# A streaming mixer layer on one core: parts of the weights kept in DRAM, one LayerNorm moved to the vector engine, and a bias added by DMA

## The chip, the cores and the metric

The program runs on one core of a Trainium2 chip. The metric is the device time of one execution in microseconds (us), as the median of several runs. TensorE (PE in the profile) does the matrix products, VectorE (DVE) and ScalarE (ACT) the elementwise work that may read PSUM, GpSimd (POOL) elementwise work in SBUF, and SyncE (SP) issues the DMAs in a queue of its own. Each engine runs its instructions in the order in which they stand.

## The reference

One post-norm layer over 2048 new frames and 8 running streams of 16 frames (17 token tiles of 128). One projection `w_in` (1024 x 2816) feeds three branches; their gated outputs are concatenated, projected by `w_out` (1024 x 1024), added to the residual and normalised.

```
h = x @ w_in ;  a, g_a, u, v, g_b, c1, c2, g_c = split(h)
y_a = pool_mixer(a)                                  # trailing means, then a small product
v_n = layer_norm(v, gmlp_ln_g, gmlp_ln_b)            # an output for the running streams
y_b = u * (tril(W_s) @ v_n + b_s)                    # chunks of 128 frames, 4 heads
y_c = pointwise(silu(layer_norm(conv31(c1 * sigmoid(c2)))))
out = concat(silu(g_a)*y_a, silu(g_b)*y_b, silu(g_c)*y_c) @ w_out + b_out
x_new = layer_norm(ALPHA * x + out, ln_g, ln_b)
```

## The kernel before, in words

All of it is float32. A product is made of three one-pass products: each operand is split into a high and a low part (`hi + lo` is the operand exactly), and `mm3` (L183 to L195) issues hi x hi, lo x hi and hi x lo for each of 8 k-tiles. `split` (L150) makes the parts: a copy on ACT (`hi`, L152) and a subtraction on DVE (`lo`).

The tokens are worked on in three blocks of 6, 6 and 5 tiles. A block goes through eight column groups of `w_in` in this order: c2/c1 (two groups), ga/a (two groups of two column tiles), v, gb, u, gc. A group's weights come in four pieces of two k-tiles: `Piece` (L166) loads one into the stage (`stage`, 4 slots) and splits it into the ring (`whi`, `wlo`, 6 slots each). `Loader` (L799) keeps the stage full while the group before runs. Every block loads and splits all of `w_in` again. The tokens `xT` are loaded and split k-tile by k-tile (`XRow`, L212) while the last group of the block before runs.

The order of every engine is written by the program itself. `Clock.pe` counts TensorE's modelled time; `after(us, fn)` puts `fn` into a list of events, and `poll` calls what is due after each k-step. `fill` holds the taps of the 31-tap convolution, one DVE instruction each (`acc<-cext,cw,acc`, with `acc<-cexts,...` for the running streams in the third block): they are put into DVE's order whenever its modelled time `Clock.dve` is behind `Clock.pe`. The order fixes only what stands behind what on an engine; when an instruction starts is decided by its waits.

Branch B (`b_v`, L627): for each token tile the v product lands in PSUM (`ps_v`), DVE makes its statistics (`vst`, `vmv`), POOL makes 1/sqrt(var + eps) and -mean times it (`vrs`, `vnm`, three instructions), ACT normalises (`vn<-ps_v`, L385), and POOL multiplies by the gain and adds the offset (L649, L650). Of every run of three tiles and for each of four heads, `vn` is then split (`vhi` on ACT, `vlo` on DVE) and multiplied with the spatial weights (`ps_z`, L672). These products stand in TensorE's order among those of group gb, from 12 us of modelled time after the run's last tile on.

The output phase: the mixed branches come back from DRAM (`mix`, `Mixed` L871) and are split (`mhi`, `mlo`); w_out is split too (`woxhi`, `woxlo`, and the ring). The first two token tiles are multiplied together, k by k, then one tile after another (`ps_o`). The residual `xr` (5 buffers) is loaded, POOL adds b_out/ALPHA to it (`add_bias`, L946), which is a 128 x 1024 tile made of a broadcast load and one scaling on POOL (L926), and DVE adds the product (`xr<-xr,ps_o`); then statistics, ACT, gain and offset on DVE, and the store. Between the first tiles stands the rest of branch C of the third block (`tail_steps`: `csum`, `ps_mean`, `dc`, `csq`, `csqs`, `ps_var`, `cvar`, `crs`, `ps_rstd`).

Of the kernel before, what the change touches and what calls it, by code (L numbers as in the profile page):

```python
# [25 lines left out]
# Column tiles of 128 of the input projection.  # L26
# [23 lines left out]

# Columns of the packed per-partition constants.
# [22 lines left out]
def encoder_kernel(ctx: ExitStack, tc: tile.TileContext, a):  # L74
# [9 lines left out]
    # Every engine runs in the order given here.  # L84
    ctx.enter_context(tc.manual_schedule())

    class Clock:
        """TensorE's time as the products are given (us), and the vector engine's; what is to follow
        later waits in `events`, and the convolution's steps in `fill` for the vector engine's free time."""
# [14 lines left out]
    def drain(tag=None):  # L104
        """What is left of the convolution that `tag` names, or all of it."""
        while fill and (tag is None or any(t == tag for t, _ in fill)):
            fill.pop(0)[1]()
# [11 lines left out]
    class Vector:  # L119
        """The vector engine, with its time counted."""  # L120
# [27 lines left out]
    ring = {}  # L148

    def split(hi, lo, src, then=None):  # L150
        """src (float32) = hi + lo exactly, both in the tensor engine's one-pass type."""
# [14 lines left out]
    class Piece:  # L166
        """A load into the stage, and later its split into a piece of the weight ring."""
        def __init__(self, key, src, cols):
            self.key, self.n, self.cols = key, src.shape[1], cols
# [3 lines left out]
        def split(self, then=None):  # L173
# [3 lines left out]
            ring.setdefault(self.key, []).append((hi, lo))  # L177

# [4 lines left out]
    def mm3(outs, kdim=KT, hook=None):  # L183
        """outs: (ps, lhs, rhs); the products of both parts but for lo x lo, below float32's last bit."""
# [18 lines left out]
    def w_in(key, g):  # L203
        """The loads of a group's weights, to be made one by one."""
        w = len(GROUPS[g]) * P
        v = a["w_in"][:, gofs[g]:gofs[g] + KT * w].rearrange("p (k c) -> p k c", k=KT)
        return [lambda k0=k0: Piece(key, v[:, k0:k0 + 2, :], w) for k0 in range(0, KT, 2)]
# [4 lines left out]
    class XRow:  # L212
        """A load of one k-tile of a block's tokens, and later its split."""
        def __init__(self, b, k, mid=None):
# [6 lines left out]
            else:  # L221
                # in two parts with another load between
# [15 lines left out]
    # keeps TensorE's clock up until the first products  # L238
# [6 lines left out]
    # the first block's loads, the first two k-tiles' weights one by one  # L245
# [33 lines left out]
    # sums over the partitions, to all of them  # L279
# [3 lines left out]
    # conv weights halved, since its input is kept doubled  # L283
# [24 lines left out]
    def load_pool():  # L308
        # two groups of 64 channels on the diagonal
# [14 lines left out]
    def keep_lower(w):  # L324
        """Spatial weights [s, h, t], kept where s <= t."""
        nc.gpsimd.affine_select(out=w, in_=w, compare_op=ALU.is_ge, fill=0.0, base=0,
                                pattern=[[0, 4], [1, P]], channel_multiplier=-1)

    after(12, load_pool)
# [7 lines left out]
    def store(q, j, src):  # L337
        """Channels of a token tile's mixed branches, from channel tile j on."""
# [8 lines left out]
    # running streams' states  # L347
# [15 lines left out]
    def stats(src, npiece, nm, then):  # L363
        """Of each row: 1/sqrt(var + eps), and -mean times it, given to `then`."""
# [11 lines left out]
    def rstd(mv, nm):  # L376
        rs = const.tile([P, 1], F32, tag="rs", bufs=4, name=nm + "rs")
        nc.gpsimd.tensor_scalar(rs, mv[:, 1:2], 1.0, EPS, op0=ALU.mult, op1=ALU.add)
        nc.gpsimd.tensor_tensor(out=rs, in0=rs, in1=mhalf, op=ALU.pow)
        nm_ = const.tile([P, 1], F32, tag="nm", bufs=4, name=nm + "nm")  # L380
# [6 lines left out]
    # weights of branch C's pointwise product  # L387
# [16 lines left out]
    def c_in(b, todo, wkey, hook=None):  # L404
        """todo: (c1 or c2, channel tile, its columns in the group); with several the products go k by k."""
# [40 lines left out]
    def conv(b, j):  # L446
# [18 lines left out]
        if T > Tp:  # L465
            # the new convolution states, at their own scale
# [29 lines left out]
    def tail_steps(b):  # L496
        """The rest of branch C in pieces of TensorE's work, each a while after the one before."""
# [16 lines left out]
        def centre(i, t0, n):  # L514
            """Less the mean, which the sums over the channels give on every partition."""
# [17 lines left out]
        def variance(i, t0, n):  # L533
            """Of each token on its partition, to the power of -1/2."""
# [77 lines left out]
    def spread(steps, every=STEP):  # L612
        """One step after another, some of TensorE's time apart."""
# [11 lines left out]
    b_state = {}  # L625

    def b_v(b, wkey, hook=None):  # L627
# [4 lines left out]
        while i < len(tiles):  # L632
# [6 lines left out]
            for r, q in enumerate(run):  # L639
# [5 lines left out]
                def norm(rs, nm_, o=vn[:, r, :], ps=ps):  # L645
                    normalise(o, ps[:, :384], rs, nm_)

                    def gain():
                        nc.gpsimd.tensor_tensor(out=o, in0=o, in1=vg, op=ALU.mult)  # L649
                        nc.gpsimd.tensor_tensor(out=o, in0=o, in1=vb, op=ALU.add)  # L650
                    after(0.8, gain)
# [442 lines left out]
```

## Time and profile before

| what | value |
|---|---|
| median of three runs | 805.1 us (805.04 to 805.83) |
| span of the profiled execution | 802.9 us, so 2.2 us of the median lie outside a span like it |
| busy: PE, DVE, ACT, POOL | 778.2, 659.0, 255.0, 216.7 us |
| DMA | 88.34 MB, mean 110 GB/s |
| mean granted TensorE clock | 0.993 |
| block 1, block 2, block 3, output phase (by the products in the timeline) | about 4 to 206, 206 to 413, 413 to 589, 589 to 794 us |

The span of the profiled execution is the only time that the page has of it. In the views, a row of the table of stretches gives the stretch, its length, then for PE, PEld, DVE, ACT and POOL the busy time with the number of instructions, then the granted clock, the DMA share and GB/s. A row of a group gives busy time, the mean of one in ns, and the idle time ahead of it with what ended it. A row of the timeline gives start, length, engine, line, operation, output<-inputs and count.

### The profile page before, as it was taken

What the parts mean: (1) busy time and instruction counts of PE and PEld (TensorE: products, weight loads), DVE (VectorE), ACT (ScalarE), POOL (GpSimd) and SP (SyncE); (2) the same over time, 40 slices, a digit from 0 to 9 for tenths busy, and PEclk for the clock granted to TensorE, in tenths of its full rate; (3) what the DMA queues carried; (4) which work ended last, traced back from release to release, by engine and by line L of the source; (5) the groups of instructions that cost most, each with busy time, mean ns of one, the idle gap of its engine ahead of it and who ended that gap; (6) DMA issues with size and microseconds to landing.
All of it is one profiled execution on the core that took longest, in us unless ns stands there. A gap on an engine that the chain in (4) does not pass through costs nothing.

```text
span 802.9 us, 11388 instructions
## 1 busy us (share of the span) xinstructions
PE 778.2 (97%) x4340; PEld 734.9 (92%) x4340; DVE 659.0 (82%) x930; ACT 255.0 (32%) x457; POOL 216.7 (27%) x226
## 2 busy tenths in 40 slices
PE   8999998999999999989999999999999899999995
PEld 6999997999999999989999999999988678888885
DVE  5998989995588999999667888999777897676665
ACT  5313224314432241431354243442351233231210
POOL 1010077300002005731000201742009344232332
PEclk9999999999999999999999999999999999999998
DMA  7513311225501253111461134222575344425321
GB/s 244 162 53 109 100 60 57 64 66 170 165 28 53 73 133 97 60 40 59 136 199 47 54 83 129 83 69 86 159 236 203 124 138 158 158 108 177 121 79 64
DMA packets 50918, 88.34 MB, mean 110 GB/s; under 512 B 13616, under 2 KB 27440, under 8 KB 50864
## 3 DMA queue, kind: packets, MB, share of 16 engines
q1 hardware_dynamic: 50864, 87.62, 33.9%
q8 instruction: 34, 0.56, 0.3%
q14 instruction: 20, 0.16, 0.1%
HBM read 69.02 MB, written 18.58 MB: 109 GB/s over the span
## 4 chain that ended last, share of the span: by engine, by line
PE 70%; DVE 13%; POOL 6%; issue 4%; DMA 4%; ACT 2%; SPq 0%; POOLq 0%; DVEq 0%; ACTq 0%
PE ps_c L189 6%; PE ps_o L189 5%; PE ps_o L191 5%; PE ps_c L190 5%; PE ps_o L190 5%; PE ps_c L191 5%; DVE acc L131 4%; PE ps_u L191 3%; PE ps_u L189 3%; PE ps_u L190 3%; PE ps_gc L191 2%; PE ps_gc L189 2%; PE ps_gc L190 2%; PE ps_ga L190 2%; PE ps_ga L189 2%
## 5 line engine op out<-in xcount | busy, mean ns | idle before, releaser
L131 DVE SCALAR_TENSOR_TENSOR acc<-cext,cw,acc 128x768 f32<-128x768 f32 (+1 forms) x270 | 265.8, 984 | 4.0
L131 DVE TENSOR_TENSOR wlo<-stage,whi 128x768 fp32r<-128x768 f32 (+1 forms) x99 | 90.0, 919 | 15.8 <-ACT whi L152 15.4
L189 PE MATMUL ps_c<-xhi,whi 128*128 128x384 f32 (+1 forms) x288 | 96.1, 334 | 0.6 <-ACT xhi L152 0.6
L190 PE MATMUL ps_c<-xlo,whi 128*128 128x384 f32 (+1 forms) x288 | 94.7, 329 | 0.9 <-DVE xlo L131 0.9
L191 PE MATMUL ps_c<-xhi,wlo 128*128 128x384 f32 (+1 forms) x288 | 94.1, 327 | 0.0
L152 ACT CAST whi<-stage 128x768 fp32r<-128x768 f32 (+1 forms) x99 | 75.4, 773 | 25.3 <-PE ps_c L190 11.8
L191 PE MATMUL ps_o<-woxhi,mlo 128*128 128x512 f32 (+1 forms) x208 | 81.5, 392 | 1.8 <-DVE mlo L131 1.8
L189 PE MATMUL ps_o<-woxhi,mhi 128*128 128x512 f32 (+1 forms) x208 | 81.9, 394 | 0.0
L190 PE MATMUL ps_o<-woxlo,mhi 128*128 128x512 f32 (+1 forms) x208 | 80.7, 388 | 0.0
L440 POOL COPY halo_c<-cext 128x30 f32<-128x30 f32 x9 | 5.1, 567 | 213.4 <-DVE cext L131 213.4
L190 PEld LDWEIGHTS ps_c<-xlo,whi 128*128 128x128 f32 x288 | 54.4, 189 | 2.4 <-DVE xlo L131 2.4
L189 PEld LDWEIGHTS ps_c<-xhi,whi 128*128 128x128 f32 x288 | 54.5, 189 | 1.4 <-ACT xhi L152 1.2
L191 PEld LDWEIGHTS ps_c<-xhi,wlo 128*128 128x128 f32 x288 | 54.3, 189 | 0.0
L385 ACT ACTIVATE xr<-xr,onm,ors 128x1024 f32<-128x1024 f32 x16 | 19.9, 1244 | 106.3 <-POOL onm L381 106.3
L191 PEld LDWEIGHTS ps_o<-woxhi,mlo 128*128 128x128 f32 x208 | 39.4, 189 | 11.0 <-DVE mlo L131 2.2
L189 PE MATMUL ps_gc<-xhi,whi 128*128 128x384 f32 (+1 forms) x144 | 47.3, 328 | 0.0
L191 PE MATMUL ps_gc<-xhi,wlo 128*128 128x384 f32 (+1 forms) x144 | 47.0, 326 | 0.0
L190 PE MATMUL ps_gc<-xlo,whi 128*128 128x384 f32 (+1 forms) x144 | 46.9, 326 | 0.0
L190 PEld LDWEIGHTS ps_o<-woxlo,mhi 128*128 128x128 f32 x208 | 39.4, 190 | 8.1
L189 PE MATMUL ps_gb<-whi,xhi 128*128 128x384 f32 x136 | 46.8, 344 | 0.0
L189 PE MATMUL ps_u<-whi,xhi 128*128 128x384 f32 x136 | 46.6, 343 | 0.0
L189 PEld LDWEIGHTS ps_o<-woxhi,mhi 128*128 128x128 f32 x208 | 39.6, 190 | 7.5
(188 smaller groups left out, 1967.1 us busy)
## 6 DMA issues: line engine op xcount, KB each, us to landing
stage<-in_w_in SPq DMA_DIRECT2D x71, 384.0 KB, 3.6
xr<-in_x_prompt SPq DMA_DIRECT2D x16, 512.0 KB, 4.9
o_y<-xr SPq DMA_DIRECT2D x16, 512.0 KB, 2.9
stage<-mix SPq DMA_DIRECT2D x17, 384.0 KB, 4.0
stage<-in_w_in SPq DMA_DIRECT2D x24, 256.0 KB, 2.7
stage<-in_xT SPq DMA_DIRECT2D x14, 384.0 KB, 3.8
mix<-yt SPq DMA_DIRECT2D x17, 192.0 KB, 1.9
mix<-mixs SPq DMA_DIRECT2D x17, 192.0 KB, 2.1
```

Source lines behind the costliest of these rows:

```text
L131: return fn(*args, **kw)
L152: nc.scalar.copy(hi, src)
L189: nc.tensor.matmul(ps, lh, rh, start=(k == 0), stop=False)
L190: nc.tensor.matmul(ps, lh, rl, start=False, stop=False)
L191: nc.tensor.matmul(ps, ll, rh, start=False, stop=(k == kdim - 1))
L385: nc.scalar.activation(out=out, in_=src, func=AF.Identity, scale=rs, bias=nm_)
L440: nc.gpsimd.tensor_copy(halo_c[:, j, :], ext[:, Tp:Tp + CONVC])
```

## The change

Three edits are made at once.

1. **Weight parts kept in DRAM.** In the first block each split piece is also stored: `put` writes `whi` and `wlo` to DRAM tiles `keep` (two DMAs of 384 KB, or 256 KB in the groups of two column tiles, 3 us of modelled time after the split; `put_first` does it for the very first piece). In the second and third block `Kept` loads both parts instead of loading and splitting a piece: into the ring, or, for the first two pieces of every second group, into the four stage slots, which TensorE then reads directly. Only the last group of the third block still goes through `Piece`. The token loads at the ends of the first and second block are put at other places, since the stage now serves the weights as well.
2. **v normalised on DVE.** DVE computes (v - mean) * gain straight from PSUM, POOL makes 1/sqrt(var + eps) (two instructions), and DVE multiplies by it and adds the offset 2.4 us of modelled time later. ACT and the other three POOL instructions drop out.
3. **The output bias by accumulating DMAs.** A small tile b_out/ALPHA of 8 x 128 is made once early and stored to DRAM (`bias`). `add_bias` becomes a DMA from POOL's queue that reads this row for all 128 partitions and adds it to `xr` in SBUF. The 128 x 1024 tile, its load and its scaling are gone.

```diff
     class Piece:
         def split(self, then=None):
...
             ring.setdefault(self.key, []).append((hi, lo))
+            if self.keep is not None:
+                after(3, lambda: put(self.keep, hi, lo, self.cols))
+
+    def put(keep, hi, lo, cols):
+        for x, part in enumerate((hi, lo)):
+            nc.sync.dma_start(out=keep[:, x], in_=part[:, :, :cols].bitcast(F32))
+
+    class Kept:
+        def __init__(self, key, k, keep, cols, staged):
+            if staged:
+                parts = [stage().bitcast(F32R).rearrange("p (k c) -> p k c", k=2) for _ in range(2)]
+            else:
+                parts = [core.tile([P, 2, 384], F32R, tag=x, bufs=RING, name=x) for x in ("whi", "wlo")]
+            for x, part in enumerate(parts):
+                nc.sync.dma_start(out=part[:, :, :cols].bitcast(F32), in_=keep[:, x])
+            ring.setdefault(key, [None] * (KT // 2))[k] = tuple(parts)
+
+    def w_kept(b, g):
+        w = len(GROUPS[g]) * P
+        return [lambda k=k: Kept((b, g), k, kept[g][k], w, g % 2 == 1 and k < 2) for k in range(KT // 2)]
...
-                def norm(rs, nm_, o=vn[:, r, :], ps=ps):
-                    normalise(o, ps[:, :384], rs, nm_)
-
-                    def gain():
-                        nc.gpsimd.tensor_tensor(out=o, in0=o, in1=vg, op=ALU.mult)
-                        nc.gpsimd.tensor_tensor(out=o, in0=o, in1=vb, op=ALU.add)
-                    after(0.8, gain)
-                stats(lambda _: ps[:, :384], 1, "v", norm)
+                st = const.tile([P, 1, 6], F32, tag="st1", bufs=4, name="vst")
+                vec.bn_stats(out=st[:, 0, :], in_=ps[:, :384])
+                mv = const.tile([P, 2], F32, tag="mv", bufs=4, name="vmv")
+                vec.bn_aggr(out=mv, in_=st.rearrange("p a b -> p (a b)"))
+                o = vn[:, r, :]
+                vec.scalar_tensor_tensor(out=o, in0=ps[:, :384], scalar=mv[:, 0:1], in1=vg,
+                                         op0=ALU.subtract, op1=ALU.mult)
+                rs = inverse(mv, "v")
+                after(2.4, lambda o=o, rs=rs: vec.scalar_tensor_tensor(out=o, in0=o, scalar=rs, in1=vb,
+                                                                       op0=ALU.mult, op1=ALU.add))
...
         for g in range(LASTG):
-            loads = Loader([(fn, 1) for fn in w_in((b, g + 1), g + 1)])
-            after(6, loads.next)
-            after(9, loads.next)
-            group_work(b, g, loads.hook({1: 1, 3: 1}))
+            if b == 0 or (b, g + 1) == (LASTB, LASTG):
...
+            else:
+                for i, fn in enumerate(w_kept(b, g + 1)):
+                    after(10 + i if g % 2 == 0 and i < 2 else 5 + i, fn)
+                group_work(b, g, None)
...
-    for nm in ("b_out", "ln_g", "ln_b"):
+    for nm in ("ln_g", "ln_b"):
...
-    nc.gpsimd.tensor_scalar(bc["b_out"], bc["b_out"], 1.0 / ALPHA, 0.0, op0=ALU.mult, op1=ALU.add)
...
     def add_bias(q):
-        nc.gpsimd.tensor_tensor(out=resid[q], in0=resid[q], in1=bc["b_out"], op=ALU.add)
+        nc.gpsimd.dma_start(out=resid[q], in_=bias.rearrange("j c -> (j c)").partition_broadcast(P),
+                            accum_op=ALU.add)
```

TensorE's order of products is the same before and after, product for product. The other engines' orders move; three places follow, in the program's names (numbers tell tiles apart and differ between the two programs).

DVE in the first block, before, from the statistics of the v group's fourth tile to the first `vlo` of the spatial products (`acc1` are taps):

```order
L131 BN_STATS vst_1141<-ps_v_1094 128x6
L131 BN_AGGR vmv_1143<-vst_1141 128x2
L131 SCALAR_TENSOR_TENSOR acc1_490<-cext1_344,cw_173,acc1_490 128x768 x4
L131 BN_STATS vst_1188<-ps_v_1145 128x6
L131 BN_AGGR vmv_1190<-vst_1188 128x2
L131 SCALAR_TENSOR_TENSOR acc1_490<-cext1_344,cw_173,acc1_490 128x768
L131 TENSOR_TENSOR vlo_1197<-vn_964,vhi_1196 128x288
```

The same place after, from the fourth tile's statistics too:

```order
L131 BN_STATS vst_1202<-ps_v_1161 128x6
L131 BN_AGGR vmv_1204<-vst_1202 128x2
L131 SCALAR_TENSOR_TENSOR vn_1160<-ps_v_1161,vmv_1204,vg_185 128x384
L131 SCALAR_TENSOR_TENSOR acc1_519<-cext1_365,cw_177,acc1_519 128x768
L131 SCALAR_TENSOR_TENSOR vn_1160<-vn_1160,vrs_1207,vb_186 128x384
L131 SCALAR_TENSOR_TENSOR acc1_519<-cext1_365,cw_177,acc1_519 128x768
L131 BN_STATS vst_1244<-ps_v_1210 128x6
L131 BN_AGGR vmv_1246<-vst_1244 128x2
L131 SCALAR_TENSOR_TENSOR vn_1160<-ps_v_1210,vmv_1246,vg_185 128x384
L131 SCALAR_TENSOR_TENSOR acc1_519<-cext1_365,cw_177,acc1_519 128x768
L131 TENSOR_TENSOR vlo_1257<-vn_1031,vhi_1256 128x288
```

Each v tile has two more DVE instructions, taps have been put later for them, and the second of the two waits for POOL's `vrs`.

POOL at the start of the output phase, before:

```order
L926 TENSOR_SCALAR b_out<-b_out 128x1024
L947 TENSOR_TENSOR xr<-xr,b_out 128x1024 x3
L378 TENSOR_SCALAR ors<-omv 128x1
L379 TENSOR_TENSOR ors<-ors,mhalf 128x1
L381 TENSOR_SCALAR onm<-omv,ors 128x1
```

and after:

```order
L1033 DMA xr<-bias 128x1024 x3
L426 TENSOR_SCALAR ors<-omv 128x1
L427 TENSOR_TENSOR ors<-ors,mhalf 128x1
L433 TENSOR_SCALAR onm<-omv,ors 128x1
L426 TENSOR_SCALAR ors<-omv 128x1
```

The scaling is gone and the three adds have become three DMA issues; the DMAs of the later tiles stand where the later adds stood.

SP in the second block, before, around the loads of the group after v (`ya`, `mixs` are stores of finished branches):

```order
L339 DMA mix_197<-ya 128x128
L171 DMA stage<-in_w_in 128x768 x4
L339 DMA mix_198<-ya 128x128
L339 DMA mix_199<-ya 128x128
L339 DMA mix_200<-ya 128x128
```

and in the changed program the loads of group v itself, which now go to the ring:

```order
L387 DMA mix_196<-mixs 128x384
L195 DMA whi<-keep_0_839 128x768
L195 DMA wlo<-keep_0_839 128x768
L195 DMA whi<-keep_2_840 128x768
L195 DMA wlo<-keep_2_840 128x768
L195 DMA whi<-keep_4_841 128x768
L195 DMA wlo<-keep_4_841 128x768
```

One load of four pieces has become eight loads, two to a piece, straight to the places from which TensorE reads.

More of the change, by code (lines that the diff above doesn't have):

```diff
@@ L166, in encoder_kernel, with __init__ @@
     class Piece:
-        def __init__(self, key, src, cols):
-            self.key, self.n, self.cols = key, src.shape[1], cols
+        def __init__(self, key, src, cols, keep=None):
+            self.key, self.n, self.cols, self.keep = key, src.shape[1], cols, keep
             self.st = stage()[:, :self.n * cols].rearrange("p (k c) -> p k c", k=self.n)
@@ L206, in w_in, with put_first @@
         v = a["w_in"][:, gofs[g]:gofs[g] + KT * w].rearrange("p (k c) -> p k c", k=KT)
-        return [lambda k0=k0: Piece(key, v[:, k0:k0 + 2, :], w) for k0 in range(0, KT, 2)]
+        if key[0] == 0:
+            kept[g] = [dram.tile([P, 2, 2, w], F32, name=f"keep{g}_{k0}") for k0 in range(0, KT, 2)]
+        keep = kept[g] if key[0] == 0 else [None] * (KT // 2)
+        return [lambda k0=k0: Piece(key, v[:, k0:k0 + 2, :], w, keep[k0 // 2]) for k0 in range(0, KT, 2)]
+    kept = {}
+    def w_kept(b, g):
+        w = len(GROUPS[g]) * P
+        return [lambda k=k: Kept((b, g), k, kept[g][k], w, g % 2 == 1 and k < 2) for k in range(KT // 2)]
+    def put_first():
+        hi, lo = ring[0, 0][0]
+        put(kept[0][0], hi, lo, 384)
     xhi = [None] * (KT // 2)
@@ L327, in keep_lower, with make_bias, scaled @@
                                 pattern=[[0, 4], [1, P]], channel_multiplier=-1)
+    after(5, put_first)
+    bias = dram.tile([KT, P], F32, name="bias")
+    def make_bias():
+        w = const.tile([KT, P], F32, name="bias_s")
+        nc.sync.dma_start(out=w, in_=a["b_out"].rearrange("(j c) -> j c", c=P))
+        def scaled():
+            nc.gpsimd.tensor_scalar(w, w, 1.0 / ALPHA, 0.0, op0=ALU.mult, op1=ALU.add)
+            after(3, lambda: nc.sync.dma_start(out=bias, in_=w))
+        after(8, scaled)
+    after(40, make_bias)
     after(12, load_pool)
@@ L374, in stats, with inverse @@
         after(1.0, rest)
-    def rstd(mv, nm):
+    def inverse(mv, nm):
         rs = const.tile([P, 1], F32, tag="rs", bufs=4, name=nm + "rs")
@@ L379, in rstd @@
         nc.gpsimd.tensor_tensor(out=rs, in0=rs, in1=mhalf, op=ALU.pow)
+        return rs
+    def rstd(mv, nm):
+        rs = inverse(mv, nm)
         nm_ = const.tile([P, 1], F32, tag="nm", bufs=4, name=nm + "nm")
@@ L852, in encoder_kernel, with leave, load @@
         for g in range(LASTG):
-            loads = Loader([(fn, 1) for fn in w_in((b, g + 1), g + 1)])
-            after(6, loads.next)
-            after(9, loads.next)
-            group_work(b, g, loads.hook({1: 1, 3: 1}))
-        if b < LASTB:
-            W = [(fn, 1) for fn in w_in((b + 1, 0), 0)]
-            X = [(lambda k=k: XRow(b + 1, k), 1) for k in range(KT)]
-            loads = Loader(W[:2] + X[:1] + W[2:3] + X[1:3] + W[3:] + X[3:])
-            group_work(b, LASTG, loads.hook({1: 1, 2: 1, 3: 2, 4: 2, 5: 2, 6: 2}))
-            loads.next(3)
-            X = None
+            if b == 0 or (b, g + 1) == (LASTB, LASTG):
+                loads = Loader([(fn, 1) for fn in w_in((b, g + 1), g + 1)])
+                after(6, loads.next)
+                after(9, loads.next)
+                group_work(b, g, loads.hook({1: 1, 3: 1}))
+            else:
+                for i, fn in enumerate(w_kept(b, g + 1)):
+                    after(10 + i if g % 2 == 0 and i < 2 else 5 + i, fn)
+                group_work(b, g, None)
+        if b == 0:
+            W = w_kept(b + 1, 0)
+            after(5, W[0])
+            after(6, W[1])
+            loads = Loader([(lambda k=k: XRow(b + 1, k), 1) for k in range(KT)])
+            def leave(k):
+                if k in (2, 4):
+                    W[1 + k // 2]()
+                if 2 <= k < 7:
+                    loads.next()
+            group_work(b, LASTG, leave)
+            loads.next(3)
+        elif b < LASTB:
+            for i, fn in enumerate(w_kept(b + 1, 0)):
+                after(5 + i, fn)
+            rows = {}
+            def load(*ks, b=b):
+                for k in ks:
+                    rows[k] = XRow(b + 1, k)
+            def leave(k):
+                if k in (2, 4):
+                    load(k - 2, k - 1)
+                if k == 5:
+                    for i in range(2):
+                        rows[i].split(lambda i=i: load(i + 4))
+            group_work(b, LASTG, leave)
+            for i in range(2, 4):
+                rows[i].split(lambda i=i: load(i + 4))
+            for i in range(4, KT):
+                after((2.5, 3.5, 5.5, 6.5)[i - 4], lambda i=i: rows[i].split())
     flush()
```

## The prediction

> **What bounds the kernel now.** I read the page first, then who waits for whom on TensorE, then the stretches of 20 us, then the timeline where stretches fall short.
>
> ```profile
> span 802.9 us, 11388 instructions
> PE 778.2 (97%) x4340; PEld 734.9 (92%) x4340; DVE 659.0 (82%) x930; ACT 255.0 (32%) x457; POOL 216.7 (27%) x226
> ...
> PE ps_z L672 <- DVE vlo L131: 6.6, 9, 1.9
> PE ps_var L538 <- DVE csqs L131: 2.1, 1, 2.1
> PE ps_o L191 <- DVE mlo L131: 1.8, 1, 1.8
> PE ps_rstd L561 <- ACT crs L555: 1.5, 1, 1.5
> ...
> PE ps_z L672 <- ACT vhi L152: 0.8, 1, 0.8
> ...
> PE tp_b L706 <- DVE yb L131: 0.5, 1, 0.5
> ```
>
> TensorE is busy 97% of the span, and its order of products does not change. So the change can win only what TensorE waits, and what its clock loses through that. The stretches show where:
>
> ```profile
> 100.00:120.00 20.00, 20.00 (x116) 19.72 (x114) 17.75 (x24) 3.81 (x7) 16.12 (x18) 1.00 0.20 60
> 120.00:140.00 20.00, 15.89 (x87) 14.57 (x87) 18.16 (x18) 9.13 (x19) 14.63 (x14) 0.99 0.17 48
> 140.00:160.00 20.00, 20.00 (x111) 20.00 (x111) 19.61 (x21) 7.55 (x14) 6.60 (x4) 0.92 0.23 73
> ...
> 400.00:420.00 20.00, 20.00 (x123) 20.00 (x123) 12.12 (x17) 11.28 (x18) 0.00 (x0) 1.00 0.65 213
> 640.00:660.00 20.00, 16.48 (x67) 12.98 (x68) 18.17 (x28) 7.86 (x16) 8.92 (x9) 0.91 0.52 172
> 700.00:720.00 20.00, 20.00 (x91) 16.70 (x90) 12.62 (x19) 5.66 (x9) 6.62 (x8) 1.00 0.39 142
> ```
>
> Undisturbed, 116 products pass in 20 us, 0.172 us from start to start. The waits lie in two kinds of place: the spatial products after group v (120 to 140, and the same place of the second block), and the first tiles of the output phase (up to 660). In or right after one of each the granted clock is below 1.
>
> Why the spatial products wait, in ACT's and POOL's rows of the first block:
>
> ```profile
> 114.39 0.67 ACT L385 ACTIVATE vn<-ps_v,vnm,vrs 128x384 f32<-128x384 f32 x1 [5.79 <-POOL vnm L381]
> 119.76 0.67 ACT L385 ACTIVATE vn<-ps_v,vnm,vrs 128x384 f32<-128x384 f32 x1 [4.70 <-POOL vnm L381]
> 120.33 0.42 ACT L152 CAST vhi<-vn 128x288 fp32r<-128x288 f32 x1
> ...
> L650 POOL TENSOR_TENSOR vn<-vn,vb 128x384 f32<-128x384 f32 x17 | 21.3, 1254 | 1.3
> L649 POOL TENSOR_TENSOR vn<-vn,vg 128x384 f32<-128x384 f32 x17 | 20.3, 1196 | 13.4 <-ACT vn L385 13.4
> L379 POOL TENSOR_TENSOR vrs<-vrs,mhalf 128x1 f32<-128x1 f32 x17 | 15.7, 924 | 1.4
> L378 POOL TENSOR_SCALAR vrs<-vmv 128x1 f32<-128x1 f32 x17 | 9.8, 575 | 21.7 <-DVE vmv L131 20.7
> ```
>
> POOL needs 5.4 us for a v tile (119.76 less 114.39), TensorE 24 x 0.172 = 4.1. POOL falls back 1.3 us a tile, ACT stands in line for a later tile's `vn`, and the ready `vhi` of the first run stands behind it. DVE waits with it, and while POOL works six taps take 8.22 us, 1.37 each, against 1.01 for one alone:
>
> ```profile
> 128.40 8.22 DVE L131 SCALAR_TENSOR_TENSOR acc<-cext,cw,acc 128x768 f32<-128x768 f32 x6
> ...
> 138.24 1.01 DVE L131 SCALAR_TENSOR_TENSOR acc<-cext,cw,acc 128x768 f32<-128x768 f32 x1
> ```
>
> The output phase starts late on DVE, since POOL scales b_out for 9.3 us and then adds it three times:
>
> ```profile
> L926 POOL TENSOR_SCALAR b_out<-b_out 128x1024 f32<-128x1024 f32 x1 | 9.3, 9341 | 55.5 <-DMA b_out<-in_b_out 55.5
> L947 POOL TENSOR_TENSOR xr<-xr,b_out 128x1024 f32<-128x1024 f32 x17 | 41.3, 2432 | 0.1
> ...
> 614.49 1.28 DVE L131 SCALAR_TENSOR_TENSOR xr<-xr,ps_o 128x512 f32<-128x512 f32 x2 [3.44 <-POOL xr L947]
> 632.88 2.98 DVE L131 TENSOR_TENSOR mlo<-stage,mhi 128x768 fp32r<-128x768 f32 x1 [0.31 <-ACT mhi L152]
> ```
>
> DVE idles 3.44 us there, and the later `mlo` of 2.98 us, beside another add, is what TensorE waits for.
>
> **What can be won.** A wait costs its idle time and a refill: a lone product takes 334 ns where one in a row takes 172, so 0.16.
>
> ```profile
> L189 PE MATMUL ps_v<-whi,xhi 128*128 128x384 f32 x136 | 45.5, 334 | 0.0
> ```
>
> - Spatial products: 6.6 + 0.8 + 10 x 0.16 = 9.0 us.
> - Output phase: 2.1 + 1.8 + 1.5 + 3 x 0.16 = 5.9 us. `yb`: 0.5 + 0.16 = 0.7 us.
> - Clock: 0.92 over 20 us is at most 1.6 us; 111 products instead of 116 are 5 x 0.172 = 0.9. I take 1.3 for it, between them, and 1.5 for the second (0.91): 2.8.
>
> Sum 18.4 us. It takes the clock's loss as a result of the waits. The Trainium skill ("TensorE: Matmul & The Clock Gate", What's actually happening) has the clock halved after an idle window of about 3.4 us; the longest wait here is 2.1, so by it these dips would come from elsewhere and stay, and the sum would be 15.6. The trace has both dips in or right behind the stretches with the waits, so I keep 18.4 and make the page's case a rival.
>
> **Part by part.**
>
> *v on DVE.* Per tile ACT loses 0.67 us, POOL keeps 0.58 + 0.92 = 1.5 of its 5.4, under TensorE's 4.1, so nothing piles up. DVE gains two instructions; no row has them, bounds are 0.55 (the statistics read as many elements) and 0.61:
>
> ```profile
> L131 DVE SCALAR_TENSOR_TENSOR ya<-ps_pool,cst,sga 128x384 f32<-128x384 f32 x10 | 6.1, 612 | 3.1 <-PE ps_pool L788 3.1
> L131 DVE BATCH_NORM_STATS2 vst<-ps_v 128x6 f32<-128x384 f32 x17 | 9.4, 555 | 0.0
> L131 DVE BATCH_NORM_AGGREGATE vmv<-vst 128x2 f32<-128x6 f32 x17 | 3.1, 182 | 0.7
> ```
>
> I take 0.61, the same operation: 12 x 0.61 = 7.3 us in the first block, which has no relief from kept weights. The cover is DVE's idle time at that block's end, 20 - 10.62 = 9.4 us:
>
> ```profile
> 180.00:200.00 20.00, 20.00 (x119) 19.93 (x118) 10.62 (x13) 7.32 (x12) 0.00 (x0) 1.00 0.51 174
> ```
>
> Whether the first `vlo` comes in time I add up along DVE's new order, from the first statistics to the first product, which would stand at 120.81 less its wait and refill, 119.9:
>
> ```profile
> 98.77 0.56 DVE L131 BATCH_NORM_STATS2 vst<-ps_v 128x6 f32<-128x384 f32 x1
> ...
> 120.81 0.40 PE L672 MATMUL ps_z<-vhi,wsthi 128*128 128x288 f32 x1 [0.76 <-ACT vhi L152]
> ```
>
> 5 statistics with aggregation 3.7, 9 new instructions 5.5, 5 taps at 1.01 5.1, 2 weight subtractions 2.0, 2 pooling splits (0.55, by their elements) and 2 `ya` 2.3, `vlo` 0.45, one full wait for POOL's pair 1.5, since no tap stands between at the first tile: 20.5, so 119.3. In time by 0.6 us. The second run has the same work in front of it and as long to do it.
>
> *Kept weights.* They remove 60 splits of at most 1.01 us on DVE (under 61 us; 16 are narrower) and as many copies on ACT, all in blocks 2 and 3, off TensorE's path except through the waits above.
>
> ```profile
> L131 DVE TENSOR_TENSOR wlo<-stage,whi 128x768 fp32r<-128x768 f32 x71 | 70.9, 1010 | 14.1 <-ACT whi L152 13.7
> ...
> stage<-in_w_in SPq DMA_DIRECT2D x71, 384.0 KB, 3.6
> ```
>
> They add 64 stores and 120 loads to SP's queue, 23 MB written and 21 MB more read. A group of three column tiles loads 3.1 MB. The row 400:420 moves 213 GB/s at 0.65 share, so about 328 at full: 9.6 us of the 24.8 that the group before lasts. On SP the loads stand behind stores of branches at worst; slots come free at the end of the group before last. I cost them at nothing, cover 10 us or more; the two-tile groups (2.1 MB, 6.4 of 16.5 us, 13.8 in block 3) are the tightest. Token splits before block 3 come later than before; I allow one wait of 0.7.
>
> *The bias.* The rows of the residual's loads and of the one broadcast load:
>
> ```profile
> 596.89 3.77 SPq L943 DMA_DIRECT2D xr<-in_x_prompt  x5
> ...
> xr<-in_x_prompt SPq DMA_DIRECT2D x16, 512.0 KB, 4.9
> b_out<-in_b_out SPq DMA_DIRECT2D x1, 512.0 KB, 7.1
> xr<-in_x_prompt SPq DMA_DIRECT2D x5, 512.0 KB, 10.2
> ```
>
> The first three adds wait for `xr` to land, median 10.2 us from issue in that burst. How long an accumulating DMA takes no row shows; below 4.9 us (a plain load of that size) is excluded by its bytes, above I take 10.2. I choose 7.1, the broadcast load, since it too reads one row for all partitions. First `xr` ready at 596.9 + 10.2 + 7.1 = 614.2, against 614.5 before; 612.0 to 617.3 at the ends. The next two, issued together with it, follow closely instead of one POOL add of 2.4 us after another, and the 768-wide `mlo`, beside no POOL add, should take 1.0 (as `wlo`) instead of 2.98. That clears the waits of 1.8 and 2.1; for the last, the 2.4 us add ahead of POOL's `cvar` is gone. I allow one remaining wait of 0.8. By the Trainium skill ("DMA: Bandwidth & Descriptors", Anatomy of one DMA) 512 KB cost 2.0 + 1.2 = 3.2 us, an estimate, which would make `xr` ready at 610.3.
>
> Sum: 802.9 - 18.4 + 0.7 + 0.8 = 786.0 span. The median lies 2.2 us above the span, so 788.2, said as 788.
>
> **The rivals.**
>
> - *First-block DVE too late* (its spare 0.6 us is thin, taps at 1.37 would eat it): the waits of that block stay, about half of 9.0 and the 1.3 clock: 788 + 6 = 794.
> - *The output waits stay*, the add by DMA landing as late as POOL's: 788 + 5.9 + 1.5 = 795.
> - *Kept weights late*, half a microsecond at each of 14 group borders, by double traffic on one queue: 788 + 14 x (0.5 + 0.16) = 797. For it: SP issues in order. Against: share 0.65 at most after 400.
> - *The dips stay* (the page's rule): 788 + 2.8 = 791.
> - *No effect*: the waits move to another late part on DVE, which stays 80% busy: 804.
> - *Slower: the accumulating DMA paces the output phase.* TensorE takes 48 x 20/91 = 10.5 us a tile. Above that, each of some 14 tiles waits. At 14 us: 14 x 3.5 = 49, so 837. It decides from 10.5 + 17/14 = 11.7 us on, where the 17 us won are lost. Against it: plain DMAs of that size land in 4.9.
>
> **How the numbers follow.** Likeliest, all waits go but one or two: 0.50. First-block waits stay 0.12, output waits stay 0.11, late weights 0.08, dips stay 0.06, no effect 0.04, slow accumulate (or kept weights so late that more than 17 us are lost) 0.09. Its own range is 785 (no new wait: 786.7, and 0.2% of scatter) to 791. 785 to 797 holds all but no effect, slow accumulate and half of late weights, some 0.17. Beyond 0.2% (1.6 us, about what a measurement can tell): faster 0.86, same 0.04, slower 0.10.
>
> **What would show it.** Right: in the waits of TensorE no `ps_z` row above 0.5 us in sum; no stretch between 40 and 780 us under 19.5 busy; clock 1.00 throughout; POOL's work in group v at 1.5 us a tile; ACT no longer waiting for `vnm`; the first `xr<-xr,ps_o` no later than 614 minus the time won before. Wrong: TensorE or its weight loads waiting for DMAs of `keep`; DVE idle before `xr` for the bias DMA; waits on `vlo` in the first block; a time of landing above 10.5 us for `xr<-bias`.

## The result, and the profile after

The changed kernel takes 786.9 us (median of four runs, 786.48 to 787.3) against 805.1 before, a ratio of 0.9777 with a 95% interval of 0.9762 to 0.9792. The forecast was 788, in a likeliest range of 785 to 791. The profiled execution has a span of 785.6 us, 17.3 less than before; 1.3 us of the median lie outside a span like it.

The page after, its first lines and its DMA packets:

```profile
span 785.6 us, 11369 instructions
PE 771.1 (98%) x4340; PEld 732.1 (93%) x4340; DVE 595.2 (76%) x904; ACT 203.8 (26%) x380; POOL 122.4 (16%) x175
...
DMA packets 77255, 141.32 MB, mean 180 GB/s; under 512 B 15872, under 2 KB 42000, under 8 KB 77200
```

DVE carries 64 us less work than before, though v gave it 34 instructions more. The traffic rose from 88.3 to 141.3 MB.

Who waits for whom on TensorE (engine, tile, line, releaser: us in total, times, longest):

```profile
PE ps_var L590 <- DVE csqs L131: 1.9, 1, 1.9
...
PE tp_b L761 <- ACT yt L763: 0.8, 1, 0.8
...
PE ps_rstd L613 <- ACT crs L607: 0.6, 1, 0.6
```

No `ps_z` row is left, and neither TensorE nor its weight loads wait for a DMA of `keep`. The stretches that waited before, and two with the stores and loads of the kept weights (the figure before the last is the DMA share), in the new kernel:

```profile
20.00:40.00 20.00, 20.00 (x118) 20.00 (x117) 14.14 (x18) 6.51 (x11) 0.72 (x2) 1.00 0.97 350
...
100.00:120.00 20.00, 20.00 (x118) 20.00 (x117) 19.35 (x35) 4.13 (x8) 3.73 (x10) 1.00 0.50 186
120.00:140.00 20.00, 20.00 (x121) 20.00 (x120) 18.04 (x24) 8.58 (x19) 4.60 (x5) 1.00 0.62 216
140.00:160.00 20.00, 20.00 (x119) 19.96 (x118) 19.58 (x20) 5.22 (x8) 4.61 (x3) 1.00 0.49 160
...
280.00:300.00 20.00, 20.00 (x117) 20.00 (x116) 17.63 (x24) 4.62 (x9) 2.52 (x4) 1.00 0.81 301
...
620.00:640.00 20.00, 17.44 (x79) 13.66 (x78) 17.95 (x28) 8.23 (x18) 5.15 (x6) 1.00 0.69 192
```

TensorE is full and its clock at 1.00 where it had been at 15.89 busy, and at 0.92 after that; the output phase still has one short stretch (620 to 640). POOL's work in 100 to 120 fell from 16.12 to 3.73 us. DVE's new instructions and POOL's two remaining ones, in the groups and in the first block's timeline:

```profile
L131 DVE SCALAR_TENSOR_TENSOR vn<-ps_v,vmv,vg 128x384 f32<-128x384 f32 x17 | 10.5, 618 | 0.8
L131 DVE SCALAR_TENSOR_TENSOR vn<-vn,vrs,vb 128x384 f32<-128x384 f32 x17 | 10.4, 613 | 0.2 <-POOL vrs L427 0.2
...
L427 POOL TENSOR_TENSOR vrs<-vrs,mhalf 128x1 f32<-128x1 f32 x17 | 9.4, 553 | 1.4
L426 POOL TENSOR_SCALAR vrs<-vmv 128x1 f32<-128x1 f32 x17 | 3.3, 193 | 71.1 <-DVE vmv L131 71.1
...
117.80 0.45 DVE L131 TENSOR_TENSOR vlo<-vn,vhi 128x288 fp32r<-128x288 f32 x1
```

They take 0.62 and 0.61 us, and the first `vlo` of the spatial products is done at 118.25.

TensorE issues the same products in the same order in all kernels, so a product's start in two traces tells how far one is ahead. In the first tile of the third block's `ps_pw`, before stands at 519.71, the changed kernel at 507.43:

```profile
519.71 0.34 PE L189 MATMUL ps_pw<-shi,pwhi 128*128 128x384 f32 x1
```

```profile
507.43 0.33 PE L208 MATMUL ps_pw<-shi,pwhi 128*128 128x384 f32 x1
```

Read so at three products (those that stand in before near 100 us, 588 and 737), the gain is 0.5 us up to 100, 11.7 in the rest of the three blocks, and 4.9 in the output phase.

### The profile page after: what moved, and what is told of

It reads as the page before. It is cut to its first block, busy times and chain, and to the rows that moved or that the text cites. A ratio compares the mean times of both kernels' runs of the same rounds, so it can differ in the third digit from the quotient of the medians.

```text
span 785.6 us, 11369 instructions
## 1 busy us (share of the span) xinstructions
PE 771.1 (98%) x4340; PEld 732.1 (93%) x4340; DVE 595.2 (76%) x904; ACT 203.8 (26%) x380; POOL 122.4 (16%) x175
## 4 chain that ended last, share of the span: by engine, by line
PE 83%; DVE 7%; DMA 5%; ACT 2%; issue 1%; POOL 1%; SPq 1%; POOLq 0%; DVEq 0%; ACTq 0%
PE ps_o L208 6%; PE ps_o L210 6%; PE ps_o L209 5%; PE ps_c L208 5%; PE ps_c L209 4%; PE ps_c L210 4%; PE ps_gb L208 3%; PE ps_gb L209 3%; PE ps_v L209 3%; PE ps_gb L210 3%; PE ps_v L210 3%; PE ps_v L208 3%; PE ps_u L210 3%; DVE acc L131 3%; PE ps_u L208 3%; PE ps_u L209 3%
## 5 line engine op out<-in xcount | busy, mean ns | idle before, releaser
L208 PE MATMUL ps_c<-xhi,whi 128*128 128x384 f32 (+1 forms) x240 | 79.7, 332 | 0.8 <-ACT xhi L152 0.7
L209 PE MATMUL ps_c<-xlo,whi 128*128 128x384 f32 (+1 forms) x240 | 78.7, 328 | 0.7 <-DVE xlo L131 0.5
L210 PE MATMUL ps_c<-xhi,wlo 128*128 128x384 f32 (+1 forms) x240 | 78.4, 327 | 0.0
L131 DVE SCALAR_TENSOR_TENSOR xr<-xr,ps_o 128x512 f32<-128x512 f32 (+1 forms) x35 | 23.1, 668 | 38.6 <-PE ps_o L210 23.1
L131 DVE TENSOR_TENSOR xlo<-stage,xhi 128x768 fp32r<-128x768 f32 (+2 forms) x26 | 21.6, 853 | 36.8 <-ACT xhi L152 36.8
L210 PE MATMUL ps_u<-whi,xlo 128*128 128x384 f32 x136 | 45.6, 335 | 0.0
L209 PE MATMUL ps_u<-wlo,xhi 128*128 128x384 f32 x136 | 45.5, 335 | 0.0
L209 PE MATMUL ps_v<-wlo,xhi 128*128 128x384 f32 x136 | 45.5, 334 | 0.0
L210 PE MATMUL ps_v<-whi,xlo 128*128 128x384 f32 x136 | 45.5, 334 | 0.0
L208 PE MATMUL ps_v<-whi,xhi 128*128 128x384 f32 x136 | 45.5, 334 | 0.0
```

The costliest lines, as they stand in the source:

```text
L131: return fn(*args, **kw)
L208: nc.tensor.matmul(ps, lh, rh, start=(k == 0), stop=False)
L209: nc.tensor.matmul(ps, lh, rl, start=False, stop=False)
L210: nc.tensor.matmul(ps, ll, rh, start=False, stop=(k == kdim - 1))
```

## The experiments

The edits come apart, so each was run alone and each pair together. The table has the median, its ratio to the kernel before on the same chip, and the gain in us by stage as above (negative: lost).

| kernel | median us | ratio, 95% interval | to 100 | blocks | output phase |
|---|---|---|---|---|---|
| v alone | 798.0 | 0.992, 0.9889 to 0.9951 | 0.1 | 12.0 | -5.0 |
| kept weights alone | 798.7 | 0.9922, 0.9895 to 0.9949 | 0.0 | -1.1 | 6.9 |
| bias alone | 798.8 | 0.9926, 0.9903 to 0.9949 | 0.7 | 0.5 | 4.0 |
| kept + bias | 799.0 | 0.9928, 0.9906 to 0.9951 | 1.1 | -0.9 | 5.1 |
| v + bias | 789.1 | 0.98, 0.9781 to 0.9818 | 0.6 | 12.0 | 3.0 |
| v + kept | 785.5 | 0.9755, 0.9735 to 0.9775 | 1.1 | 11.8 | 6.5 |
| all three | 786.9 | 0.9777, 0.9762 to 0.9792 | 0.5 | 11.7 | 4.9 |
| v + kept, once more | 785.1 | 0.9762, 0.9735 to 0.9789 | 0.7 | 11.8 | 6.8 |
| all three, once more | 787.2 | 0.9784, 0.9757 to 0.9811 | 0.6 | 11.7 | 6.0 |

The first column lies ahead of the first v tile and differs between two runs of one kernel (1.1 and 0.7); I take it for scatter in the landing of the first loads, which no run tests. Two traces of the changed kernel differ by 1.1 us in the output phase, so smaller differences there say little. The first two gains of a row, added, tell how far TensorE is ahead when the output phase begins; a time of that phase plus this sum is called its time on the clock of the kernel before.

**v alone.** The kernel before with the second edit:

```diff
-                def norm(...): normalise(...); after(0.8, gain)
-                stats(lambda _: ps[:, :384], 1, "v", norm)
+                vec.scalar_tensor_tensor(out=o, in0=ps[:, :384], scalar=mv[:, 0:1], in1=vg, ...)
+                after(2.4, lambda ...: vec.scalar_tensor_tensor(out=o, in0=o, scalar=rs, in1=vb, ...))
-TAILQ = 9
+TAILQ = 2
```

(DVE's modelled time is now behind by a few taps at output tile 2; the second number lets the third block's tail begin there, as it does in the other kernels.)

> The kernel before with the v edit alone. Theory: POOL's 5.4 us a v tile is what made the spatial products wait, and taking it down is enough. TensorE then gains what the changed kernel gained by the end of its third block (11.4 us of the two traces' difference between 66 us and the first output tiles, the clock's dip in the first block included), and the output phase keeps its waits: 805.1 - 11.4 = 794, with no ps_z wait above 0.5 us in sum and waits of mlo, csqs and crs near 1.8, 2.1 and 1.5 us. Rival (DVE, full with weight splits in all blocks, is what must be relieved, and two more instructions a v tile overload it): waits of ps_z on vlo stay or grow in the second block, 799 to 806.

798.0, not 794. The blocks came out as the theory has it, 12.0 us, and no `ps_z` row is left. But the output phase didn't stay as it was: it lost 5.0. TensorE's waits, and POOL and DVE there:

```profile
PE ps_o L210 <- DVE mlo L131: 6.3, 2, 5.9
PE ps_var L585 <- DVE csqs L131: 2.1, 1, 2.1
...
590.54 13.09 POOL L976 TENSOR_SCALAR b_out<-b_out 128x1024 f32<-128x1024 f32 x1 [56.20 <-DVE acc L131]
...
602.37 0.35 DVE L131 SCALAR_TENSOR_TENSOR acc<-cexts,cw,acc 128x128 f32<-128x128 f32 x1
606.15 1.28 DVE L131 SCALAR_TENSOR_TENSOR xr<-xr,ps_o 128x512 f32<-128x512 f32 x2 [3.44 <-POOL xr L997]
```

POOL's scaling of b_out took 13.1 us here and ended at 603.63, 0.91 after DVE's last tap of the row (602.72). In the kernel before it ended 0.92 after it:

```profile
602.63 9.34 POOL L926 TENSOR_SCALAR b_out<-b_out 128x1024 f32<-128x1024 f32 x1 [55.47 <-DMA b_out<-in_b_out]
...
610.71 0.34 DVE L131 SCALAR_TENSOR_TENSOR acc<-cexts,cw,acc 128x128 f32<-128x128 f32 x1
```

So most of the 9.3 us wasn't POOL's work but standing behind DVE's row of taps (with DVE idle the scaling takes 1.05, as the next run shows), and v on DVE had made that row longer: 13 pairs of taps from the scaling's start against 9. The first add of `xr` came 3.8 us later than in the kernel before (606.15 is 618.3 on its clock, against 614.49).

**Kept weights alone.** The kernel before with the first edit, in short:

```diff
-            loads = Loader([(fn, 1) for fn in w_in((b, g + 1), g + 1)])
+            for i, fn in enumerate(w_kept(b, g + 1)): after(..., fn)
```

> The kernel before with the kept weights alone. Theory: POOL still needs 5.4 us a v tile and ACT still stands behind it, so the first block stays as it is (7 us of waits and clock), and in the second block only what DVE and ACT are relieved of can shorten the waits: a gain of 0 to 3 us, 802 to 805. Rival (the weight splits on DVE and ACT are what makes the spatial products late): the second and third block's ps_z waits of about 4 us go, and the stalls at mlo and csqs shrink as DVE comes early into the output phase: 799 or less. Second rival (the traffic of the loads delays TensorE): waits on DMAs of keep, above 806.

798.7, outside the theory's 802 to 805, and the rival is half right. The spatial products wait a little longer than before, 8.8 us against 7.4, and the blocks lose 1.1:

```profile
PE ps_z L724 <- DVE vlo L131: 6.1, 5, 1.7
PE ps_z L724 <- ACT vhi L152: 2.7, 1, 2.7
...
602.38 1.05 POOL L1010 TENSOR_SCALAR b_out<-b_out 128x1024 f32<-128x1024 f32 x1 [46.25 <-DMA b_out<-in_b_out]
...
610.33 2.67 DVE L131 SCALAR_TENSOR_TENSOR xr<-xr,ps_o 128x512 f32<-128x512 f32 x4 [10.54 <-PE ps_o L210]
```

But DVE, relieved of the splits, had put its taps behind it by then. The scaling took 1.05 us, the first adds of `xr` waited for TensorE alone and came 5.2 us earlier in the phase (610.33 is 609.25 on the clock of the kernel before), `mlo` and `csqs` left the list of waits, and the one on `crs` fell to 0.6. These 4.8 us of waits, two refills of 0.16 and the dip of the clock that went with them (1.5 in the prediction's sum) come to 6.6 of the 6.9 us. TensorE waited for no DMA of `keep`, so the second rival is out.

**Bias alone.** The kernel before with the third edit (`add_bias` as a DMA, no tile and no scaling).

> The kernel before with the bias edit alone. Theory: the output phase gains what it gained in the changed kernel (5.1 us between its first tiles and its end), the blocks keep their waits: 800, with the first add of xr on DVE about as early after the phase's start as in the changed kernel, mlo near 1 us, one wait on csqs of about 2 us, and no dip of the clock in this phase. Rival (DVE comes into the output phase late because of taps and splits, and the bias alone doesn't help): the wait on mlo stays, 803 to 805.

798.8, near the 800 expected: 4.0 us in the output phase, with csqs at 1.9 and a small rest of mlo. The scaling is gone here too, but the first add of `xr` came no earlier for it: it waited for the accumulating DMA, and 613.17 is 614.4 on the clock of the kernel before, where it stood at 614.49. What was won lies behind it. The later pair of `mlo`, beside no POOL add, took 1.29 us instead of 3.32, and with no add of 2.4 us ahead of POOL's `cvar` the wait on `crs` is gone; these are steps that the prediction names. One thing expected did not come: the phase has a dip of the clock, 3.4 us at half right behind the wait on csqs (0.98 and 0.94 in the stretches from 620 and 640).

```profile
PE ps_z L721 <- DVE vlo L131: 5.9, 8, 1.9
PE ps_var L586 <- DVE csqs L131: 1.9, 1, 1.9
...
PE ps_o L210 <- DVE mlo L131: 0.3, 1, 0.3
...
613.17 1.28 DVE L131 SCALAR_TENSOR_TENSOR xr<-xr,ps_o 128x512 f32<-128x512 f32 x2 [3.61 <-DMA xr<-bias]
...
631.43 1.29 DVE L131 TENSOR_TENSOR mlo<-stage,mhi 128x768 fp32r<-128x768 f32 x2 [0.31 <-ACT mhi L152]
```

**Kept weights and bias, no v.**

> The changed kernel with v normalised as before (ACT and POOL's pair). Theory: the first block's waits and dip come back in full (7 us), those of the second block in part (0 to 4 us), the output phase stays improved: 794 to 798. Rival (kept weights did it): below 791.

799.0, 1 us above the range. The `ps_z` waits are back in full (8.6 us), and in the output phase the two edits together bring 5.1, not the 10.9 of their gains alone. DVE, early through the kept weights, sat idle for 14.53 us until the accumulating DMA landed and made its first add at 614.13, which is 614.3 on the clock of the kernel before. So the DMA's landing takes back the early start that kept weights give.

**v and bias, no kept weights** (and `TAILQ = 2` as above).

> The changed kernel without the kept weights (the third block's tail is made to begin with the third output tile, as it does in both kernels). Theory: kept weights do nothing for the spatial products, so the three blocks gain their 11.9 us as with v alone; but DVE then carries taps into the output phase, two more per cent than before, and the 6.1 us wait on mlo that v alone brought is shortened only by what the bias DMAs bring (about 4 us, since DVE then waits neither for the scaling nor for the adds): waits of about 2 us on mlo and 2 on csqs, 788.5 to 791. Rival (kept weights are only cover, and cost and gain nothing): 786.5 to 788.

789.1, as expected: the blocks gain 12.0 without any kept weight, and the waits in the output phase are those forecast:

```profile
PE ps_var L586 <- DVE csqs L131: 1.9, 1, 1.9
...
PE ps_o L210 <- DVE mlo L131: 1.4, 1, 1.4
```

**v and kept weights, no bias edit.** POOL scales b_out and adds it, as before.

```diff
-        nc.gpsimd.dma_start(out=resid[q], in_=bias....partition_broadcast(P), accum_op=ALU.add)
+        nc.gpsimd.tensor_tensor(out=resid[q], in0=resid[q], in1=bc["b_out"], op=ALU.add)
```

> The changed kernel with the bias as before (a scaled 128 x 1024 tile, added by POOL). Theory, formed from the runs so far: POOL's scaling took 9.3 us only because DVE's taps ran beside it (1.05 us in the kernel with kept weights alone, where DVE had finished), so with kept weights the bias edit has nothing left to remove; the first add of xr waits for TensorE alone, and the waits on mlo and csqs go: 784 to 787.5, with the scaling near 1 us. Rival, the prediction's own reckoning: the bias edit is worth 5 us, and without it the waits on mlo, csqs and crs are back: 791 to 793.

785.5, under the changed kernel itself; the prediction's reckoning would have had 792. The scaling took 1.05 us and the first residual add came 5.5 us earlier than with the DMA (4.9 counted from the phase's own beginning, 0.6 earlier here). Two details were not as expected: it waited for POOL's first add and not for TensorE alone, and a wait of 1.0 us on crs stayed.

```profile
590.49 1.05 POOL L1012 TENSOR_SCALAR b_out<-b_out 128x1024 f32<-128x1024 f32 x1 [57.50 <-DMA b_out<-in_b_out]
...
596.75 1.28 DVE L131 SCALAR_TENSOR_TENSOR xr<-xr,ps_o 128x512 f32<-128x512 f32 x2 [9.45 <-POOL xr L1033]
```

The same place in the changed kernel, where DVE waits for the accumulating DMA. The line on landings is of the first three, which are issued one after another here; the last line has the median of all 17:

```profile
592.46 2.10 POOL L1033 DMA_DIRECT2D xr<-bias  x2 [58.90 <-DMA xr<-in_x_prompt]
...
DMA to landing us min/median/max: 9.7/11.1/12.2
...
602.27 1.28 DVE L131 SCALAR_TENSOR_TENSOR xr<-xr,ps_o 128x512 f32<-128x512 f32 x2 [14.12 <-DMA xr<-bias]
...
xr<-bias POOLq DMA_DIRECT2D x17, 512.0 KB, 5.2
```

**POOL's pair left out.** The kernel before without the multiplication and addition of v's gain and offset on POOL:

```diff
-                    def gain(): ...
-                    after(0.8, gain)
```

> The kernel before with POOL's multiplication and addition on vn left out (v is normalised, without gain and offset); all else as before, ACT's normalisation too, and no instruction more on DVE. Theory: the spatial products wait because POOL needs 5.4 us a v tile against TensorE's 4.1; without the pair it needs about 3, so the ps_z waits and the first block's dip go: 11 to 12 us less, 792 to 794, the output phase as before. Rival (ACT's part of the chain, vn normalised there, or DVE's load is the cause): ps_z waits stay at more than half, 799 or more.

792.9 (0.9834, 0.9806 to 0.9862), with 11.9 us in the blocks and no `ps_z` row, although ACT's `vn<-ps_v` and DVE's order stayed. The first block's six `vn` on ACT, from 102.54 to 130.63 in the kernel before (5.6 us apart in the mean), now stand 4.1 apart, which is TensorE's pace:

```profile
102.03 0.67 ACT L385 ACTIVATE vn<-ps_v,vnm,vrs 128x384 f32<-128x384 f32 x1 [8.82 <-POOL vnm L381]
...
122.68 0.66 ACT L385 ACTIVATE vn<-ps_v,vnm,vrs 128x384 f32<-128x384 f32 x1
```

So it is POOL's load, as a rate, that made the spatial products wait, and not ACT's place in the chain. The output phase lost 0.9 us, with 2.7 of waits on mlo. POOL and DVE met there in another order, which shows both sides of it:

```profile
589.73 1.17 POOL L922 TENSOR_SCALAR b_out<-b_out 128x1024 f32<-128x1024 f32 x1 [55.58 <-DVE acc L131]
593.62 7.68 POOL L943 TENSOR_TENSOR xr<-xr,b_out 128x1024 f32<-128x1024 f32 x3 [2.72 <-DMA xr<-in_x_prompt]
...
593.74 2.89 DVE L131 SCALAR_TENSOR_TENSOR acc<-cext,cw,acc 128x512 f32<-128x512 f32 x1
596.56 2.49 DVE L131 SCALAR_TENSOR_TENSOR acc<-cexts,cw,acc 128x128 f32<-128x128 f32 x1
```

Here POOL got its turn in the middle of the taps, and three taps of 0.74 and 0.34 us took 2.89, 2.49 and 2.89, a POOL add each. That the scaling ended with taps still to come also shows that it needs nothing from them.

**b_out scaled early.** The kernel before, with the scaled row made early and loaded for all partitions, and POOL's adds kept:

```diff
-    nc.gpsimd.tensor_scalar(bc["b_out"], bc["b_out"], 1.0 / ALPHA, 0.0, ...)
+        src = bias.rearrange("j c -> (j c)") if nm == "b_out" else a[nm]
```

> The kernel before with one piece of the bias edit: b_out is scaled early as a small tile and its scaled row is loaded for all partitions, so that POOL's 9.3 us scaling is gone, but POOL still adds it to xr, 2.4 us each. Theory: the scaling is what held up DVE's first adds; then this is worth nearly what the accumulating DMAs are (799 measured with them alone): 798 to 801, first add of xr when TensorE and DVE's taps are done, 611 to 612 less what went before. Rival (POOL's adds, which slow DVE's two-input operations, are the cost): the waits on mlo and csqs stay at over 3 us together, 802 to 804.

801.1 (0.9946, 0.9928 to 0.9965): by the time at the theory's upper end, but its mechanism fails. The output phase gains 2.2 of the 4.0 that the DMAs brought, and the waits on csqs and mlo stay at 2.1 and 1.2, as the rival has them. Now the first POOL add is what stands behind the taps:

```profile
606.80 11.01 POOL L996 TENSOR_TENSOR xr<-xr,b_out 128x1024 f32<-128x1024 f32 x3 [60.33 <-DMA xr<-in_x_prompt]
...
610.45 0.34 DVE L131 SCALAR_TENSOR_TENSOR acc<-cexts,cw,acc 128x128 f32<-128x128 f32 x1
613.09 1.28 DVE L131 SCALAR_TENSOR_TENSOR xr<-xr,ps_o 128x512 f32<-128x512 f32 x2 [2.30 <-POOL xr L996]
```

So it is not the scaling as such: here the add that comes first pays in its place.

**Four on one chip.** The changed kernel once more, v + kept once more, and two attempts at a faster one.

> The changed kernel as it is, once more, beside the next three on one chip: 786.9 as measured first, within 0.5 us.

787.2 (0.9784, 0.9757 to 0.9811), 786.02 to 787.64.

> The changed kernel with the bias as before, once more, beside the changed kernel. Theory: with kept weights the accumulating DMAs bring the first residual tile later (602.3 in the trace, waited for from 588) than POOL's scaling and adds do (596.8); that makes csqs late, 2.1 us. So this stays 1 to 2.5 us under the changed kernel. Rival (the 1.4 us between the two came from two chips): the two are within 0.5 us.

785.1 (0.9762, 0.9735 to 0.9789), 784.77 to 786.16, so 2.0 us under the changed kernel beside it, with ranges that overlap by 0.1. The wait on csqs is gone in both traces of it and there in both of the changed kernel; a wait on crs is in all four (1.0 and 0.9 against 0.6). The size of the wait on csqs, 1.9 in one trace and 1.1 in the other, goes with the landing of the first accumulating DMA: DVE's first add is at 602.27 and at 600.74.

> The changed kernel with the first three residual tiles' bias added by POOL, from a row that was scaled early and is loaded for all partitions, and the other tiles' by accumulating DMAs. Theory: the first adds come as early as with POOL alone, so no wait on csqs, and POOL's adds no longer stretch the later mlo (3.3 us beside an add, 1.3 for two splits without): as without the bias edit or up to 1 us less, 783.5 to 785.5. Rival (the accumulating DMAs cost something in every tile): 786 to 787.5.

784.5 (0.9752, 0.9726 to 0.9778), 784.30 to 784.73: every run under every run of the changed kernel, and the fastest here; its output phase gains 8.5 us against the 6.0 of the changed kernel beside it. The edit, beside the row loaded as in the kernel above:

```diff
+        if q < 3:
+            nc.gpsimd.tensor_tensor(out=resid[q], in0=resid[q], in1=bc["b_out"], op=ALU.add)
+        else:
+            nc.gpsimd.dma_start(out=resid[q], ..., accum_op=ALU.add)
```

The waits of TensorE that the view still lists, in the whole span, are those of the start and `tp_b`:

```profile
PE wps L277 <- POOL wz L274: 1.5, 1, 1.5
PE tp_b L761 <- ACT yt L763: 0.8, 1, 0.8
PE ps_c L208 <- ACT xhi L152: 0.7, 2, 0.5
PE ps_c L209 <- DVE xlo L131: 0.5, 1, 0.5
```

> The changed kernel with one number changed: the gain and offset of output tile 2 are put 6 us after its normalisation instead of 1.2, so that they stand behind dc and csqs on DVE and not in front. Theory: the wait on csqs (2.1 us with its refill) is those two instructions of 1.23 us, standing in DVE's order ahead of what TensorE needs; it goes, nothing else becomes late: 784.5 to 785.5. Rival (DVE is late by the DMA's landing and the order doesn't matter, or the next wait on crs takes its place): 786.3 or more.

```diff
-                after({0: 6, 1: 15}.get(q, 1.2), gain)
+                after({0: 6, 1: 15, 2: 6}.get(q, 1.2), gain)
```

786.4 (0.9779, 0.9754 to 0.9803), 785.69 to 787.71: no difference that these runs can tell. The wait on csqs went, and others took its place, as the rival says:

```profile
PE ps_rstd L613 <- ACT crs L607: 1.5, 1, 1.5
...
PE ps_o L210 <- DVE mlo L131: 1.2, 2, 0.8
```

DVE was late as a whole from its first `xr` add on (601.95 in this trace). Moving two instructions only chooses which product sees it.

## Why the prediction was right, point by point

- *TensorE's waits and clock are all there is to win.* Right. 17.3 us of span against a forecast of 16.9.
- *Spatial products, 9.0 + 1.3.* Right in place and cause, a little small: 11.7 in the blocks, where the forecast adds up to 10.3 (with 0.7 for `yb`, less 0.7 allowed for the token splits). The run without POOL's pair shows the cause by itself. The Trainium skill ("SBUF — State Buffer", SBUF: two separate sides) has POOL and a DVE instruction with two SBUF inputs hold one pair of ports in turn, each for a whole instruction, and not share it; the taps of 2.49 and 2.89 us beside POOL's adds agree. The six taps that I had read as slowed to 1.37 each are three of 1.01 and three of 1.65 to 1.68, as turns would have it.
- *v on DVE, 0.61 an instruction, first `vlo` in time by 0.6 us.* Right: 0.618 and 0.613. The first `vlo` was done at 118.25, against the 119.3 of my sum and the 119.9 at which it was needed; 0.5 us of that is TensorE's earlier start in this trace. POOL's two instructions took 0.75 us a tile and not 1.5.
- *Kept weights cost nothing and, outside the waits on POOL, bring nothing.* The first half held: no wait of TensorE on `keep`, though the DMA share reached 0.97 where the first block stores and 0.81 where the second block loads. The second half is the step that failed. I counted 61 us of splits off DVE and let none of it count for the output phase; there they bring 6.9 us alone, and with v they turn its loss of 5.0 into a gain of 6.5.
- *The bias edit wins the output phase, 5.9 + 1.5 less 0.8.* Alone it brings 4.0 of these 6.6, by two of the steps named: `mlo` beside no POOL add, and no add ahead of `cvar`. The wait on csqs was not cleared (2.1 to 1.9), and a dip stayed. What failed is the reading of the row of 9.3 us as POOL's own work: it was 1.05 of work and 8.3 of standing behind DVE's taps. So kept weights, which clear the taps away early, win the same phase by another way, and the gains do not add. With kept weights in place the accumulating DMA costs time: 6.5 without it and 4.9 with it in one pair of traces, 6.8 and 6.0 in the other. The comparison that was missing is with POOL's way once DVE is free (first add at 596.75, not 602.27).
- *First `xr` ready at 596.9 + 10.2 + 7.1 = 614.2.* Less the 12.2 us won before, that is 602.0, and the trace has the landing at 602.2. This is luck: the load was issued at 583.73, 1.0 earlier than by the sum, POOL's DMA followed it after 8.7 instead of 10.2, and that DMA took 9.7 instead of 7.1. The estimate of 3.2 us that stands beside it lies under all 17 landings (least 4.9).
- *One wait of 0.8 left there, 0.7 in the blocks.* In its place csqs 1.9 and crs 0.6 idle, and the 0.7 of `tp_b` which I had counted as won stayed (0.8 idle); the 0.7 allowed for the token splits did not come. The blocks gained 11.7 for 10.3 and the output phase 4.9 for 6.6: the errors nearly cancel, so that the time came out better than its parts is luck.
- *The dips of the clock go with the waits.* They went with them here: 1.00 in every stretch up to 780. But a wait doesn't bring a dip each time. In the kernel before the longest, 2.1 on csqs, has none behind it (clock 1.00 from 642 to 654); the bias alone has the first block's waits nearly unchanged and no dip there; the changed kernel has the 1.9 us wait and none behind it. The Trainium skill ("TensorE: Matmul & The Clock Gate", What's actually happening) asks for an idle window of about 3.4 us; the dips before stood right behind waits of 1.9 us (`vlo`) and 1.5 us (`crs`), so the traces disagree, and the rival that they stay fell. The Trainium skill adds there that the window runs freely; that would make a dip partly chance, as the missing ones suggest, but no run here tests it.
- *The rival of a slow accumulating DMA.* As a pace for the whole phase it fell: 5.2 us median from issue to landing, against the 10.5 us of a tile. But the first three took 9.7, 11.1 and 12.2, and DVE's start into the phase hangs on the first.
- *The signs.* Two that were named as signs of being wrong came in the output phase: DVE idle for the bias DMA before `xr` (14.12 us), and landings above 10.5 us (two of 17). Of those for being right, the stretches 620 to 640 (17.44 busy) and 540 to 560 (19.23) fell short.

## What to carry to other kernels

A long duration on POOL beside a busy DVE is to be compared with the same instruction where DVE is idle before it is called work: 9.3, 13.1 and 1.05 us were one instruction. Edits that bear on the same phase need not add (6.9 and 4.0 alone, 5.1 together), so their combinations have to be measured, and one of three may cost. Work taken from an engine that is "not the bound" can pay two stages later, at the point where its backlog meets the critical path.

## What the hardware showed that was not expected

A single POOL instruction stood behind an unbroken row of DVE taps, some 9 pairs of them in the kernel before and 13 in the one with v alone, and ran 0.92 and 0.91 us past the last one's end; in another kernel POOL got in between two taps of such a row. The lock that the Trainium skill describes in the section named above is held for an instruction; why the turn did not pass at the end of the next tap is open.

The accumulating DMA (512 KB, one row read for 128 partitions) landed 5.2 us after its issue in the median, and 9.7 to 12.2 us for the first three, issued within 2.7 us; why these took longer no run isolates. Each occupied POOL's queue for about 0.9 us, where the add that it replaces took 2.43.
